# A projection and merge written as one stream, with VectorE, ScalarE and DMA issue pinned to program order

## The chip, the cores and the metric

One Trainium2 chip, one core. The metric is the device time of one launch in microseconds (us), as a median over runs.

## The reference, cut to what matters

One decoder layer, float32, on 1024 prompt rows and 8 x 8 sample rows, which stand together as T = 1088 rows (544, HALF, in each half; 272, CH, in each quarter).

```python
proj = jnp.einsum('bld,de->ble', x, w_in)                 # D = 2048 -> 84 column blocks of 128
gb, gc, h, z_c, q, k, v, z_a, gate_c, gate_a = jnp.split(proj, ...)
conv_out, conv_state = short_conv(gc * h, conv_prev, conv_w)
y_c = silu(z_c) * gb * conv_out
o = window_attention(q, k, v, sinks)      # 128 keys back, ALiBi, 16 heads, 4 kv heads
y_a = silu(z_a) * o
merged = sigmoid(gate_c) * (y_c @ w_conv_out) + sigmoid(gate_a) * (y_a @ w_attn_out)
y = layer_norm(ALPHA * x + merged @ w_out)
```

## The kernel before, in words

Every product is a float32 one in three passes: `split` (L131, L132) takes a tile apart, ScalarE (ACT) casts the high part, VectorE (DVE) subtracts it for the low one, and TensorE (PE) multiplies high by high, high by low and low by high.

A **unit** makes two column blocks of 128 for all rows from one half of the contraction, by a Strassen-Winograd scheme of 7 products (**leaves**). A leaf has 4 **groups** (one for each 128 of the contraction) of 6 matmuls 128x272, so a unit has 28 groups and 168 matmuls. Before a leaf its weights are combined on DVE (L242 to L247) and split; after it `take` adds its sum into the result (DVE, L264) or copies it where it is the first (ACT, L262). The sums of a unit lie in three PSUM tiles called a, c and b; a serves leaves 0, 2, 4 and 6, b serves 3 and 5, so a leaf's `take` has to be done before the leaf that uses its tile again. The side work shares two small PSUM tiles (`aux`).

The order of units: psa0 to psa41 over the first half of x, whose results go to DRAM (pd; psa0 and psa1 together, in `first`, L290 on). Then psb0 to psb41 over the second half, each starting from its loaded pd tile (cb): two for keys and values, eight for queries, nine gates, sixteen for the convolution with gates between them, three gates. Then 16 merge units psm (eight with w_conv_out, whose results go to DRAM as cmd; eight with w_attn_out), each quarter of whose result is multiplied by a gate loaded from sgd (L757); the second eight add the loaded cmd (cmo, L761) and store mgd (L762). Last the product with w_out and the layer norm.

The operands of a set (x0 for psa, x1 for psb, xm0 and xm1 for the merges; the names xa, xb, xm) are made in `Operands`: `load_all` loads four quarters of 4 tiles each (tags a, d, c, b; L165), `combine` makes two sums of them (L182, L183), two more sums follow at L199 and L202, and each leaf's tiles are split. The loads of x1 are issued when unit psa37 begins, those of xm0 and xm1 some units before their first use.

Side work (64 attention steps, one begun every 15 groups; 8 sample steps; the convolution; the gates) is put between groups by `at`, which runs a function when a given group has been written: an attention step is a load, 14 groups later the scores with the whole softmax, 28 the values' load, 30 the transposes, 40 the output. The order on PE is the program's own (`in_order`). On DVE, ACT and the DMA queue of SyncE (SP) it is the tile scheduler's, which takes what it holds to be ready.

Of the kernel before, what the change touches and what calls it, by code (L numbers as in the profile page):

```python
# [50 lines left out]
def tile_hybrid_step(  # L51
# [32 lines left out]


    agenda = {}
    clock = [0]

    def at(step, what):
        assert step >= clock[0]  # L90
        agenda.setdefault(step, []).append(what)

    def tick():
        clock[0] += 1
        for what in agenda.pop(clock[0], ()):
            what()

    last_pe = [None]

    def in_order(ins):  # L100

        if last_pe[0] is not None:
            tc.add_manual_dep(
                ins.ins, last_pe[0].ins.name,
                mybir.DependencyInfo(mybir.DependencyClass.NoSync, mybir.DependencyReason.DATA),
                reason="in_order",
            )
        last_pe[0] = ins

    def matmul(*args, **kw):  # L110
        in_order(nc.tensor.matmul(*args, **kw))  # L111

    def transpose(*args):
        in_order(nc.tensor.transpose(*args))  # L114

    turn_of_sum = [0]

    def sums(name):

        r = turn_of_sum[0]  # L120
        turn_of_sum[0] += 1
        return [
            ps.tile([P, 2, 512], F32, name=f"{name}{s}", tag=f"sum{(r + i) % 3}", bufs=1)
            for i, s in enumerate("acb")
        ]

    def aux(name):
        return ps.tile([P, 512], F32, name=name, tag="ax", bufs=2)
# [6 lines left out]
    nc.vector.memset(eps, LN_EPS)  # L135
# [13 lines left out]
    class Operands:  # L149
# [5 lines left out]
        def __init__(self, stage, name, sources):  # L155
            self.stage, self.name, self.sources = stage, name, sources
            self.x = [[None] * 4 for _ in range(7)]

        def load(self, r, c, tag):

            out = []
            for k, src in enumerate(self.sources):
                t = self.stage.tile([P, HALF], F32, name=f"x{tag}{self.name}{k}{r}{c}", tag=f"x{tag}{k}")
                tc.keep_in_program_order(
                    nc.sync.dma_start(t, src[r][:, c * HALF : (c + 1) * HALF])  # L165
                )
                out.append(t)
            return out

        def load_all(self, between=lambda: None):  # L170
# [4 lines left out]
            self.b22 = self.load(1, 1, "c")  # L175
            self.b12 = self.load(0, 1, "b")

        def combine(self):

            self.t3, self.t2 = self.b12, self.b22  # L180
            for k in range(4):
                nc.vector.tensor_sub(self.t3[k], self.t2[k], self.t3[k])  # L182
                nc.vector.tensor_add(self.t2[k], self.t3[k], self.b11[k])  # L183
            self.b22 = None

        def put(self, i, src):
            for k in range(4):
                o = slot([2, HALF], F32R, f"x{self.name}{i}_{k}")
                split(o[:, 0], o[:, 1], src[k])
                self.x[i][k] = o  # L190

        def step(self, i):

            if i == 2 and self.b22:
                self.combine()
            if i == 4:

                for k in range(4):
                    nc.vector.tensor_sub(self.t3[k], self.b22[k], self.t2[k])  # L199
            if i == 5:  # L200
                for k in range(4):
                    nc.vector.tensor_sub(self.b21[k], self.b21[k], self.t2[k])  # L202
            self.put(
                i,
                (lambda: self.b11, lambda: self.b21, lambda: self.t2, lambda: self.t3,
                 lambda: self.t3, lambda: self.b21, lambda: self.b22)[i](),
            )
            if i == 3:
                self.b22 = self.load(1, 1, "a")

    def enter(x, *units):

        for i in range(7):
            x.step(i)
            for u in units:
                next(u)
        for u in units:
            assert next(u, None) is None
# [5 lines left out]
    def unit(*args):  # L224
        for _ in products(*args):
            pass

    def products(name, src, x, c, add, accs=None, s=None):

        if len(src.shape) == 3:  # L230
            raw = src
        else:
            raw = upool.tile([P, 4, 512], F32, name=f"wr{name}", tag="wr", bufs=2)
            nc.sync.dma_start(raw.rearrange("p a b -> p (a b)"), src)
        a11, a21, a12, a22 = (raw[:, i] for i in range(4))
        if s is None:
            s = upool.tile([P, 2, 512], F32, name=f"ws{name}", tag="ws", bufs=1)
        s1, s2 = s[:, 0], s[:, 1]

        def ready(i):  # L240
            if i == 2:
                nc.vector.tensor_add(s1, a21, a22)  # L242
                nc.vector.tensor_sub(s2, s1, a11)
            if i == 3:
                nc.vector.tensor_sub(a21, a11, a21)
            if i == 6:
                nc.vector.tensor_sub(a12, a12, s2)  # L247
            w = wpool.tile([P, 2, 512], F32R, name=f"w{name}_{i}", tag="w", bufs=5)
            split(w[:, 0], w[:, 1], (a11, a12, s2, a21, s1, a22, a12)[i])
            return w  # L250

        acc_a, acc_c, acc_b = accs or sums(f"ps{name}")
        accs = (acc_a, acc_c, acc_a, acc_b, acc_a, acc_b, acc_a)
        starts = (True, True, False, True, False, False, False)

        def view(f, h):
            return c[:, f, h * HALF : (h + 1) * HALF].rearrange("p (a b) -> p a b", a=2)

        def take(f, h, acc, fresh):
            dst, val = view(f, h), acc[:, :, :CH]  # L260
            if fresh and not add:
                nc.scalar.copy(dst, val)  # L262
            else:
                nc.vector.tensor_add(dst, dst, val)  # L264

        after = (
            (0, 0, acc_a, True), (0, 0, acc_c, False), (1, 0, acc_a, True), (1, 1, acc_b, True),
            (1, 1, acc_a, False), (1, 0, acc_b, False), (0, 1, acc_a, True),
        )
        for i in range(7):  # L270
            w, acc = ready(i), accs[i]
            for k in range(4):
                ks = slice(k * P, (k + 1) * P)
                xo = x[i][k]
                first, last = starts[i] and k == 0, k == 3
                for wi, xi in ((0, 0), (0, 1), (1, 0)):
                    for h in range(2):
                        matmul(
                            acc[:, h, :CH], w[:, wi, ks], xo[:, xi, h * CH : (h + 1) * CH],
                            start=first and wi == 0 and xi == 0, stop=last and wi == 1,  # L280
                            skip_group_check=not starts[i],
                        )
                tick()
            take(*after[i])
            yield


    st = ExitStack()
    stage = pool("stage", stack=st, side="right")
    x0 = Operands(stage, "a", [(xt[k], xt[k + 8]) for k in range(4)])  # L290
    with ExitStack() as first:
        ps0 = pool("ps0", space=PSUM, stack=first)
        fpool = pool("first", stack=first, side="right")
        acc = [ps0.tile([P, 2, 512], F32, name=f"first{i}", tag=f"first{i}") for i in range(4)]

        idle = fpool.tile([P, 2, 512], F32, name="idle", tag="idle")
        nc.vector.memset(idle, 0.0)
        for i in range(WARM):
            matmul(acc[0][:, 0], idle[:, 0, 0:P], idle[:, 0], start=True, stop=True)

        c = [upool.tile([P, 2, T], F32, name=f"ca{p}", tag="c", bufs=2) for p in range(2)]
        raws = []

        def first_weights():
            p = len(raws)
            raws.append(upool.tile([P, 4, 512], F32, name=f"wra{p}", tag="wr", bufs=2))
            nc.sync.dma_start(raws[p].rearrange("p a b -> p (a b)"), win[p, 0])

        x0.load_all(first_weights)
        s1 = fpool.tile([P, 2, 512], F32, name="wsa1", tag="idle")  # L310
        both = [
            products(f"a{p}", raws[p], x0.x, c[p], False, (acc[2 * p], acc[2 * p + 1], acc[2 * p + 1]), (None, s1)[p])
            for p in range(2)
        ]
        enter(x0, *both)
        for p in range(2):
            nc.sync.dma_start(pd[p], c[p])
    ps = pool("ps", space=PSUM)
    x1 = Operands(stage, "b", [(xt[k], xt[k + 8]) for k in range(4, 8)])
# [721 lines left out]
```

## Time and profile before

| | |
|---|---|
| median of 3 runs | 2726.57 us (2725.57 to 2728.25) |
| the profiled execution's own time | 2730.23 us, its span 2728.5 us |
| PE busy | 2635.7 us (97%), 19426 matmuls |
| DVE busy | 1751.0 us (64%) |
| ACT busy | 1076.7 us (39%) |
| DMA | 415.99 MB, mean 152 GB/s |

Busy times are of the profiled execution. PE is busy nearly all the time, and its matmuls are pipelined, so what can be lost or won in it is its idle time and the time in which the chip grants it a lower clock (PEclk, a share of full speed). In the rows of a timeline the first two numbers are the start and the length in us, and a bracket gives the idle time before the instruction and what ended it.

### The profile page before, as it was taken

The page shows a single profiled execution, that of the slowest core. Times are in us where ns is not written, and L with a number is a line of the kernel's source. Part 1 is how long each engine was busy: PE and PEld are TensorE (multiplying, and loading weights), DVE is VectorE, ACT ScalarE, POOL GpSimd, SP SyncE. Part 2 cuts the span into 40 slices and gives each one's busy share as a digit, 9 for nine tenths or more (in the row PEclk, how much of TensorE's full clock was granted, in tenths as well). Part 3 has the DMA queues.
Part 4 walks back from the last instruction along what each step waited for, and adds up shares of the span by engine and source line. Part 5 has one row for each costly group of instructions (what it writes and reads, how often), then busy time and mean ns, then how long its engine had stood idle before and what let it go on. Part 6 is the DMA issues. An engine that isn't in the chain of part 4 may idle for free. (4 is left out here: it accounts for less than half of the span.)

```text
span 2728.5 us, 48044 instructions
## 1 busy us (share of the span) xinstructions
PE 2635.7 (97%) x19426; PEld 2546.2 (93%) x19426; DVE 1751.0 (64%) x3311; ACT 1076.7 (39%) x2070; POOL 0.2 (0%) x4
## 2 busy tenths in 40 slices
PE   7999999999999989989999999999999999899998
PEld 6999999999999989988999999999999999688886
DVE  7444444444445858877878888878866866533836
ACT  4333233332333535556664544554433523322221
POOL 0000000000000000000000000000000000000000
PEclk8999999999999999999999999999999999999999
DMA  4322222222233456665554444445446566733543
GB/s 148 121 104 112 96 96 113 109 98 96 113 124 149 145 180 211 210 192 164 184 180 153 160 150 167 143 157 194 150 163 227 171 235 204 240 100 111 181 144 104
DMA packets 167330, 415.99 MB, mean 152 GB/s; under 512 B 23442, under 2 KB 75666, under 8 KB 139172
## 3 DMA queue, kind: packets, MB, share of 16 engines
q1 hardware_dynamic: 167108, 412.92, 44.3%
q8 instruction: 153, 2.51, 0.4%
q14 instruction: 69, 0.57, 0.1%
HBM read 295.33 MB, written 119.48 MB: 152 GB/s over the span
## 5 line engine op out<-in xcount | busy, mean ns | idle before, releaser
L111 PE MATMUL o<-wo,m 128*128 128x512 f32 x1344 | 320.9, 394 | 0.2 <-DVE r L854 0.2
L111 PEld LDWEIGHTS o<-wo,m 128*128 128x128 f32 x1344 | 255.3, 190 | 55.8 <-issue 0.6
L132 DVE TENSOR_TENSOR wa<-wra,wa 128x512 fp32r<-128x512 f32 x210 | 145.4, 693 | 216.1 <-ACT wa L131 216.1
L131 ACT CAST wb<-wrb 128x512 fp32r<-128x512 f32 x210 | 129.7, 619 | 247.9 <-PE psb3b L111 12.1
L131 ACT CAST wa<-wra 128x512 fp32r<-128x512 f32 x210 | 130.4, 622 | 180.1 <-PE first L111 5.4
L132 DVE TENSOR_TENSOR wo<-wraw,wo 128x512 fp32r<-128x512 f32 x112 | 76.7, 687 | 148.7 <-ACT wo L131 148.6
L131 ACT CAST wo<-wraw 128x512 fp32r<-128x512 f32 x112 | 69.3, 621 | 223.5 <-PE o L111 188.6
L132 DVE TENSOR_TENSOR wb<-wrb,wb 128x512 fp32r<-128x512 f32 x210 | 144.4, 688 | 10.1 <-ACT wb L131 9.1
L132 DVE TENSOR_TENSOR wa<-wsa,wa 128x512 fp32r<-128x512 f32 x84 | 58.2, 693 | 109.9 <-ACT wa L131 109.9
L131 ACT CAST wa<-wsa 128x512 fp32r<-128x512 f32 x84 | 52.3, 623 | 77.8 <-issue 75.1
L132 DVE TENSOR_TENSOR wm<-wrm,wm 128x512 fp32r<-128x512 f32 x80 | 55.3, 693 | 39.8 <-ACT wm L131 39.5
L131 ACT CAST wb<-wsb 128x512 fp32r<-128x512 f32 x84 | 51.8, 617 | 56.4 <-PE psb22a L111 3.6
L131 ACT CAST wm<-wrm 128x512 fp32r<-128x512 f32 x80 | 49.7, 622 | 58.5 <-PE psm_6b L111 4.8
L473 ACT ACTIVATE p<-p,nm 128x256 f32<-128x256 f32 (+1 forms) x128 | 62.4, 488 | 23.0 <-DVE nm L465 22.7
L480 ACT ACTIVATE p<-p,den 128x256 f32<-128x256 f32 (+1 forms) x128 | 56.4, 487 | 29.1 <-DVE den L478 28.4
L111 PEld LDWEIGHTS first<-xa,wa 128*128 128x128 f32 x336 | 48.2, 212 | 17.7 <-DVE xa L132 9.3
L111 PE MATMUL first<-xa,wa 128*128 128x272 f32 x336 | 49.9, 314 | 14.7 <-DVE xa L132 8.4
L757 DVE TENSOR_TENSOR cm<-cm,sg 128x544 f32<-128x544 f32 x64 | 46.1, 723 | 27.6 <-ACT cm L262 20.3
L132 DVE TENSOR_TENSOR wb<-wsb,wb 128x512 fp32r<-128x512 f32 x84 | 57.6, 686 | 9.1 <-ACT wb L131 9.0
L131 ACT CAST pp<-pt 128x512 fp32r<-128x512 f32 (+1 forms) x64 | 35.8, 560 | 59.1 <-PE pt L114 58.5
L459 DVE SCALAR_TENSOR_TENSOR p<-delta,sc 128x256 f32<-128x256 f32 (+1 forms) x128 | 45.7, 397 | 13.4 <-PE sc L111 13.4
L111 PE MATMUL o<-wo,ms 128*128 128x512 f32 x128 | 40.5, 398 | 13.9 <-DVE ms L132 10.7
(1081 smaller groups left out, 6506.8 us busy)
## 6 DMA issues: line engine op xcount, KB each, us to landing
pd<-ca SPq DMA_DIRECT2D x42, 1088.0 KB
cb<-pd SPq DMA_DIRECT2D x42, 1088.0 KB
wra<-in_win SPq DMA_DIRECT2D x42, 1024.0 KB
wrb<-in_win SPq DMA_DIRECT2D x42, 1024.0 KB
wraw<-in_wo SPq DMA_DIRECT2D x128, 256.0 KB
sgd<-cb SPq DMA_DIRECT2D x16, 1088.0 KB
sg<-sgd SPq DMA_DIRECT2D x64, 272.0 KB
qt<-qd SPq DMA_DIRECT2D x128, 128.0 KB
```

The source lines that it names most:

```text
L111: in_order(nc.tensor.matmul(*args, **kw))
L131: nc.scalar.copy(hi, raw)
L132: nc.vector.tensor_sub(lo, raw, hi.bitcast(F32))
L459: nc.vector.scalar_tensor_tensor(p[:, e, :nk], delta[:, 2 * P - nk :], SLOPES[2 * j + e], sc[:, e, :nk], op0=ALU.mult, op1=ALU.add,)
L473: nc.scalar.activation(p[:, e, :nk], p[:, e, :nk], AF.Exp, bias=nm[:, e : e + 1], accum_out=den[:, e : e + 1],)
L480: nc.scalar.mul(p[:, e, :nk], p[:, e, :nk], den[:, e : e + 1])
L757: nc.vector.tensor_mul(c[:, f, hs], c[:, f, hs], sg)
```

## The change

What it does:

- Four wrappers (`te`, `ve`, `se`, `dq`) issue everything up to the product with w_out, and chain each instruction to the one before it on its engine: PE, DVE, ACT and SP's DMA issue are all in program order.
- All units from psa0 to psm's last are one list of (unit, leaf), walked by one loop (`run`). In leaf g: after group 0 the `take` of leaf g-1; after group 1 the weights' sums and casts of the leaf 3 ahead; after group 2 the next unit's raw weights (in leaf 0) or its result tile and pd load (in leaf 4); after group 3 the weights' low parts.
- The next operand set is made as pieces in a list `line`, of which each group takes one (two in the first two units). A set's leaf is split as soon as the last unit of the set before has done with that leaf. `ahead_of` issues a set's loads and puts the four pairs of its combination on `line` in the same moment: for x1 when psa37 begins, for xm0 when gate 13 begins, for xm1 in merge unit 4.
- Side work has fixed groups: of an attention step load 0, scores 14, bias 16, maximum 17, exponents 19, sums 22, values' load 22, scaling 23, transposes 27, high 29, low 30, output 34, then 36, 37 and 38. Long DVE instructions are cut in halves (some 68 more). The convolution's first tap goes from DVE to ACT. The sample step's loads are issued 12 groups before its first product.
- In the first two units leaves 0 and 1 of psa0 come before those of psa1; then they alternate. On DVE the last row of leaf 2's operands (xa split from xca) is now the 33rd behind the memsets, and was the 51st.
- In the merge, gate tiles are fetched one or two leaves ahead into two buffers; the weight tiles of the last stage have three buffers and had four.

```diff
+    te, ve, se, dq = (InOrder(e) for e in (nc.tensor, nc.vector, nc.scalar, nc.sync))
     def tick():
         clock[0] += 1
         for what in agenda.pop(clock[0], ()):
             what()
+        for _ in range(pieces[0]):
+            if line:
+                line.pop(0)()
-    def split(hi, lo, raw):
-        nc.scalar.copy(hi, raw)
-        nc.vector.tensor_sub(lo, raw, hi.bitcast(F32))
+        def combine(self, k):
+            line.append(lambda: ve.tensor_sub(self.t3[k], self.t2[k], self.t3[k]))
+            line.append(lambda: ve.tensor_add(self.t2[k], self.t3[k], self.b11[k]))
+            for k in range(4):
+                u.products(i, k)
+                if k == 0:
+                    settle()
+                if k == 1:
+                    todo = make_high(g + 1 + ahead(g), 2)
+                if k == 2 and nxt and i == u.loads_next and nxt.raw is None:
+                    nxt.load()
+                if k == 2 and nxt and i == 4 and nxt.c is None:
+                    nxt.room()
+                if k == 3:
+                    for v, n in todo:
+                        v.low(n)
+                tick()
+            pending[0] = (u, i)
+            if u.ops.leaves and u.ops.leaves[0] is u:
+                u.ops.leaves[1].put(i)
+    stream = [(u, i) for u in both for i in range(2)] + [(u, i) for i in range(2, 7) for u in both]
+    def ahead_of(ops):
+        ops.load_all()
+        for k in range(4):
+            ops.combine(k)
+            for dt, what in (
+                (0, self.load), (14, self.scores), (16, self.biased), (17, self.maximum),
+                (19, self.exponents), (22, self.sums), (23, self.normed), (22, self.load_values),
+                (27, self.turn), (29, self.high), (30, self.low), (34, self.output),
+                (36, self.half), (37, self.joined), (38, self.gated),
+            ):
+                at(t + dt, what)
```

How it moves instructions, at two places. In the names, wa is a weight tile split for a psa unit (its second number is the leaf), wra and wsa are the raw weights and their sums, ca is a unit's result, xbb and xcb are x1's loaded tiles of tags b and c.

DVE where x1 is combined, in unit psa37; before:

```order
L264 TENSOR_TENSOR ca_8077<-ca_8077,psa37c 128x544
L132 TENSOR_TENSOR wa_6_8256<-wra_8078,wa_6_8256 128x512
L132 TENSOR_TENSOR wa_0_8292<-wra_8286,wa_0_8292 128x512
L132 TENSOR_TENSOR wa_1_8320<-wra_8286,wa_1_8320 128x512
L247 TENSOR_TENSOR wra_8286<-wra_8286,wsa_8288 128x512
L264 TENSOR_TENSOR ca_8077<-ca_8077,psa37a 128x544
L132 TENSOR_TENSOR wa_2_8350<-wsa_8288,wa_2_8350 128x512
L182 TENSOR_TENSOR xbb_8061<-xcb_8053,xbb_8061 128x544
L182 TENSOR_TENSOR xbb_8063<-xcb_8055,xbb_8063 128x544
L183 TENSOR_TENSOR xcb_8053<-xbb_8061,xab_8037 128x544
```

The first xbb row stood behind the takes of leaf 1 (psa37c) and leaf 4 (psa37a) of psa37.

DVE at the same place, now:

```order
L97 TENSOR_TENSOR xbb_8076<-xcb_8068,xbb_8076 128x544
L97 TENSOR_TENSOR wra_7868<-wra_7868 128x512
L97 TENSOR_TENSOR xcb_8068<-xbb_8076,xab_8052 128x544
L97 TENSOR_TENSOR xbb_8078<-xcb_8070,xbb_8078 128x544
L97 TENSOR_TENSOR wa_3_8101<-wra_7868,wa_3_8101 128x512
L97 TENSOR_TENSOR xcb_8070<-xbb_8078,xab_8054 128x544
L97 TENSOR_TENSOR xbb_8080<-xcb_8072,xbb_8080 128x544
L97 TENSOR_TENSOR xcb_8072<-xbb_8080,xab_8056 128x544
L97 TENSOR_TENSOR xbb_8082<-xcb_8074,xbb_8082 128x544
L97 TENSOR_TENSOR wa_4_8135<-wsa_8032,wa_4_8135 128x512
L97 TENSOR_TENSOR xcb_8074<-xbb_8082,xab_8058 128x544
L97 TENSOR_TENSOR ca_7983<-ca_7983,psa37c 128x544
```

The first xbb row has moved ahead of psa37's take of leaf 1, and the sum wra that leaf 3's weights need (the row after it) and leaf 3's low part (wa_3) stand behind it.

SP where the sample outputs are stored (out_k_p to out_v_s) in the first sample steps; before:

```order
L437 DMA qt_6_12359<-qd_146 64x512 x2
L420 DMA szd_160<-sz_12125 128x1024
L439 DMA kt_6_12362<-ksd_137 128x256
L411 DMA qd_152<-qa_12116 64x8x128 x2
L411 DMA qd_152<-qb_12117 64x8x128 x2
L360 DMA cb_12515<-pd_74 128x2176
L587 DMA sbias_0_12139<-in_sbias 32x136
L589 DMA skt_0_12141<-in_ckt 64x4x128
L595 DMA sva_0_12144<-in_cv 128x4x64
L558 DMA out_k_p<-kl 128x256
L562 DMA out_k_s<-kn 8x256 x2
L507 DMA yd_114<-o_3_12256 128x128
```

The operands of step 6 (qt_6, kt_6), which its scores need 14 groups later, were issued before the outputs.

SP there, now:

```order
L97 DMA vt_4_12349<-vcd_141 128x256
L97 DMA szt_4_12351<-szd_154 128x128
L97 DMA yd_114<-o_3_12344 128x128
L97 DMA out_k_p<-kl 128x256
L97 DMA out_v_p<-vlast 128x256
L97 DMA out_k_s<-kn 8x256 x8
L97 DMA out_k_s<-in_ck 8x2x15360
L97 DMA out_v_s<-vn 8x256 x8
L97 DMA out_v_s<-in_cv 8x2x15360
L97 DMA qt_6_12464<-qd_146 64x512 x2
L97 DMA kt_6_12467<-ksd_137 128x256
```

Of them qt_6 and kt_6 now come behind all the outputs, the two copies of 8x2x15360 (in_ck, in_cv) among them.

## Rows read from the trace of the kernel before

**Rows 1.** The page: span, busy time by engine, chain of waits by engine.

```profile
span 2728.5 us, 48044 instructions
PE 2635.7 (97%) x19426; PEld 2546.2 (93%) x19426; DVE 1751.0 (64%) x3311; ACT 1076.7 (39%) x2070; POOL 0.2 (0%) x4
PE 12%; DMA 2%; DVE 1%; ACT 0%; issue 0%; SPq 0%; DVEq 0%; ACTq 0%
```

**Rows 2.** Windows: stretch, length, busy (count) by engine, PEclk, DMA share, GB/s.

```profile
60.00:893.00 833.00, 833.00 (x6637) 833.00 (x6636) 384.28 (x563) 251.69 (x433) 0.00 (x0) 1.00 0.29 110
945.00:1200.00 255.00, 235.59 (x1847) 233.00 (x1846) 188.74 (x396) 131.74 (x266) 0.00 (x0) 0.97 0.64 195
1200.00:1420.00 220.00, 212.26 (x1656) 203.38 (x1655) 175.75 (x503) 140.01 (x325) 0.00 (x0) 0.98 0.54 180
1420.00:1945.00 525.00, 517.03 (x4111) 513.18 (x4110) 432.69 (x897) 248.69 (x517) 0.00 (x0) 1.00 0.48 165
```

**Rows 3.** Timeline of PE, then of DVE, in the first two units.

```profile
33.28 1.73 PE L111 MATMUL first<-xa,wa 128*128 128x272 f32 x6 [6.15 <-DVE xa L132]
39.01 21.19 PE L111 MATMUL first<-xa,wa 128*128 128x272 f32 x145 [2.09 <-DVE xa L132]
...
18.77 0.69 DVE L132 TENSOR_TENSOR wa<-wsa,wa 128x512 fp32r<-128x512 f32 x1
45.84 0.74 DVE L132 TENSOR_TENSOR xa<-xba,xa 128x544 fp32r<-128x544 f32 x1
```

**Rows 4.** Timeline of SP and DVE: x1's loads in psa37, xm1's in the merge.

```profile
809.30 0.32 SPq L323 DMA_DIRECT2D pd<-ca  x1
809.67 3.16 SPq L165 DMA_DIRECT2D xab<-in_xt  x4
825.04 1.35 DVE L182 TENSOR_TENSOR xbb<-xcb,xbb 128x544 f32<-128x544 f32 x2
...
2081.37 3.19 SPq L165 DMA_DIRECT2D xam<-yd  x4
2096.70 1.45 DVE L182 TENSOR_TENSOR xbm<-xcm,xbm 128x544 f32<-128x544 f32 x2 [0.64 <-DMA xbm<-yd]
```

**Rows 5.** Timeline of PE: stalls at x1's entry and in the query and sample steps.

```profile
925.80 4.75 PE L111 MATMUL psb0a<-xb,wb 128*128 128x272 f32 x24 [3.36 <-DVE cb L264]
995.86 3.25 PE L111 MATMUL psb3a<-xb,wb 128*128 128x272 f32 x24 [3.28 <-DVE cb L264]
1007.24 1.12 PE L111 MATMUL sc<-kt,qt 128*128 128x128 f32 x4 [5.87 <-DMA qt<-qd]
1181.50 1.08 PE L111 MATMUL sps<-skt,sqs 64*32 64x136 f32 x4 [6.53 <-DMA skt<-in_ckt]
```

**Rows 6.** Timeline of SP around the sample outputs.

```profile
1177.26 0.50 SPq L558 DMA_DIRECT2D out_k_p<-kl  x1
1183.81 8.05 SPq L562 DMA_DIRECT2D out_v_s<-vn  x8
1199.34 0.33 SPq L439 DMA_DIRECT2D kt<-ksd  x1
```

**Rows 7.** Timeline of PE: waits for the shared small sums in the sample steps.

```profile
1260.15 0.40 PE L111 MATMUL spo<-spn,vn 32*64 32x128 f32 x2 [1.60 <-DVE o L503]
1294.92 1.23 PE L111 MATMUL sc<-kt,qt 128*128 128x256 f32 x4 [2.53 <-ACT so L652]
```

**Rows 8.** Timeline of PE: entries of xm0 and of xm1.

```profile
1964.32 3.25 PE L111 MATMUL psb25b<-xb,wb 128*128 128x272 f32 x24 [2.43 <-DVE cb L264]
2142.64 3.28 PE L111 MATMUL psm_7a<-xm,wm 128*128 128x272 f32 x24 [2.80 <-DVE cm L264]
```

**Rows 9.** Timeline of DVE, SP and PE at the merge's end.

```profile
2322.20 0.72 DVE L761 TENSOR_TENSOR cm<-cm,cmo 128x544 f32<-128x544 f32 x1 [1.35 <-DMA cmo<-cmd]
2328.86 0.33 SPq L905 DMA_DIRECT2D gB<-in_ln_g  x1
2323.21 1.19 PE L111 MATMUL o<-wo,ms 128*128 128x512 f32 x2 [7.77 <-DVE ms L132]
```

More of the change, by code (lines that the diff above doesn't have):

```diff
@@ L192, in step @@
[L192 to L206, printed above, removed]
-            )
-            if i == 3:
-                self.b22 = self.load(1, 1, "a")
@@ L211, in enter @@
[L211 to L285, printed above, removed]
@@ L288, in tile_hybrid_step @@
[L288 to L317, printed above, removed]
@@ L355, in tile_hybrid_step @@
[L355 to L371 removed]
+            self.t2 = self.load(1, 1, "c")
@@ new lines, in tile_hybrid_step @@
+    stage_st = ExitStack()
+    stage = pool("stage", stack=stage_st, side="right")
+    x0 = Operands(stage, "a", [(xt[k], xt[k + 8]) for k in range(4)])
+    first = ExitStack()
+    ps0 = pool("ps0", space=PSUM, stack=first)
+    fpool = pool("first", stack=first, side="right")
+    acc = [ps0.tile([P, 2, 512], F32, name=f"first{i}", tag=f"first{i}") for i in range(4)]
+    idle = fpool.tile([P, 2, 512], F32, name="idle", tag="idle")
+    ve.memset(idle, 0.0)
+    for i in range(WARM):
+        te.matmul(acc[0][:, 0], idle[:, 0, 0:P], idle[:, 0], start=True, stop=True)
@@ new lines, in tile_hybrid_step, with others @@
+    both = [
+        Unit(f"a{p}", win[p, 0], x0, end=lambda c, p=p: dq.dma_start(pd[p], c)) for p in range(2)
+    ]
+    rest = iter(both)
+    x0.load_all(lambda: next(rest).load())
+    for p, u in enumerate(both):
+        u.accs = (acc[2 * p], acc[2 * p + 1], acc[2 * p + 1])
+    both[1].loads_next = 5
+    both[1].s = fpool.tile([P, 2, 512], F32, name="wsa1", tag="idle")
+    x0.put(0)
+    x0.put(1)
+    def others():
+        x0.put(2, x0.combine)
+        for i in range(3, 7):
+            x0.put(i)
@@ new lines, in output, with heads @@
+        def output():
+            po = box["po"] = aux(f"spo{n}")
+            te.matmul(po[0:64, 0:P], vn[new, g // 2, half], pn[new], start=True, stop=False)
+            for b in range(NH):
+                c = slice(b * 32, (b + 1) * 32)
+                te.matmul(po[0:64, c], va[:, b, :], pa[:, c], start=False, stop=b == NH - 1)
+        def heads():
+            pov = box["po"][0:64, 0:P].rearrange("p (b h t) -> p b h t", b=NH, h=4)
+            for h in range(4):
+                e = h % 2
+                se.copy(o[64 * e : 64 * e + 64, h // 2], pov[:, :, h, :])
@@ new lines, in gated @@
+        def gated():
+            for jj in range(2):
+                j = 2 * g + jj
+                z = szs[:, j, new]
+                ve.tensor_mul(z, z, o[:, jj].rearrange("p b t -> p (b t)"))
+                if hb:
+                    dq.dma_start(yd[8 + j][:, 0:TS], szs[:, j, :])
+        for dt, what in (
+            (9, rows), (12, lambda: scores(0)), (15, lambda: scores(2)), (18, maximum), (20, exponents),
+            (24, sums_), (25, lambda: normed(0)), (26, lambda: normed(2)),
+            (27, lambda: turn(0)), (28, lambda: turn(1)), (29, lambda: turn(2)), (30, lambda: turn(3)),
+            (31, turn_new), (34, output), (36, heads), (38, gated),
+        ):
+            after(dt, what)
@@ L725, in tile_hybrid_step @@
-        for ct in range(8):
-            conv(ct)
-            if ct == 7:
-                at(clock[0] + 4, lambda: conv_state(0))
-                at(clock[0] + 8, lambda: conv_state(1))
-            if ct % 2:
-                gate(9 + ct // 2)
-    assert not agenda
-    keep.close()
-    mp = pool("merge", side="right")
-    st = ExitStack()
-    stage = pool("mstage", stack=st, side="right")
-    def branch(b):
-        x = Operands(stage, f"m{b}", [(yd[8 * b + k], yd[8 * b + k + 4]) for k in range(4)])
-        x.load_all()
-        x.combine()
-        return x
@@ new lines, in tile_hybrid_step, with gate_unit, samples, open_conv @@
+    for j in range(8):
+        project(QZ + j, lambda c, j=j: asked(j, c))
+    def gate_unit(d, begin=None):
+        return project(GT + d, lambda c: gate(d, c), begin)
+    def samples(i):
+        if i == 0:
+            heads_st.close()
+            open_samples()
+        sample(i // 2, i % 2)
+    for i in range(8):
+        gate_unit(i, lambda i=i: after(16, lambda: samples(i)))
+    gate_unit(8)
+    def open_conv():
+        sam.close()
+        pools["conv"] = cp = pool("conv", stack=con)
+        late["pts"] = cp.tile([18, 8, P], F32, name="cst")
@@ new lines, in tile_hybrid_step, with mix, open_merge @@
+    for ct in range(8):
+        project(CV + 2 * ct, lambda c, ct=ct: convolved(ct, c), (lambda: after(24, open_conv)) if ct == 0 else None)
+        def mix(c, ct=ct):
+            mixed(ct, c)
+            if ct == 7:
+                after(4, lambda: conv_state(0))
+                after(8, lambda: conv_state(1))
+        project(CV + 2 * ct + 1, mix)
+        if ct % 2:
+            gate_unit(9 + ct // 2)
+    mst = ExitStack()
+    xm = [None, None]
+    def open_merge():
+        con.close()
+        keep.close()
+        pools["merge"] = pool("merge", side="right")
+        stage = pool("mstage", stack=mst, side="right")
+        for b in range(2):
+            xm[b].stage = stage
+        ahead_of(xm[0])
```

921 lines of the change are left out of this document (565 added, 356 removed).

## The prediction

> **What bounds the kernel now.** I read the page first [rows 1]: PE is busy 2635.7 of 2728.5 us and leads the chain of waits, so the change can win only what PE loses: its idle time and the time at the low clock. It adds no matmul and takes none away.
>
> The windows show where PE loses [rows 2]. From 60 to 893 us 6637 matmuls take 833.00 us: 0.1255 us each, 3.01 us for a leaf of 24 matmuls, 0.753 for a group of six, no loss. In the second half I count as lost the idle time and the clock's deficit: 945 to 1200 us loses 19.4 + 0.03 x 255 = 27 us, 1200 to 1420 us 7.7 + 0.02 x 220 = 12 us, 1420 to 1945 us 8 us. That is 47 us beside the attention, the samples and the convolution. The rest I read in the timeline of PE with the releaser of each wait: the first two units wait for split operands [rows 3], and the entry of each new operand set for DVE's takes [rows 5, 8]; at the merge's end PE waits 7.77 us for ms [rows 9].
>
> The price of a wait: a leaf's 24 matmuls behind an idle time of 3.36 us took 4.75 us and not 3.01 [rows 5], so the clock adds 1.7 us to a wait of some length.
>
> **First two units.** DVE is the limit: from 18.77 to 45.84 us it starts 45 instructions, 0.62 us each [rows 3]. The last operand of leaf 2 comes 18 instructions sooner in its order, so up to 18 x 0.62 = 11 us. PE waits 6.15 and 2.09 us there for such operands [rows 3]; I take both and a little low clock, **8.5 us** won. If the later leaves' operands then come late, 4; at most 11.
>
> **Entry of x1 and of xm0.** Splitting one piece per group, as the last unit of the old set gives its slots back, spreads what came in a burst. At psb0 the wait was 3.36 us with 1.7 of clock [rows 5]: I take 4 of it. At xm0's entry the wait shown is 2.43 us [rows 8] with the clock behind it: 3. Together **7 us** won (2 to 9).
>
> **Queries, samples, convolution.** Psb3 waits 3.28 us for a take and 5.87 for its qt; the first sample step 6.53 us for skt [rows 5]. With two clock prices that is 19 of the 27 us. Skt is now issued 12 groups ahead, at least 9 us; the qt load stands behind fewer stores. I let all three go and 3 us of smaller waits, **22 us** (8 to 25).
>
> Against this stands SP's order. All stores of the sample outputs now come ahead of qt and kt of step 6. Before, SP began them at 1177.26 us, spent 8.05 us on one group of eight alone, and issued the next kt at 1199.34 us [rows 6]: 22 us. The step's scores come 14 groups later, 10.5 us and with side work some 14. So PE waits 22 - 14 = 8 us and pays 1.7 of clock: **9.7 us** lost (0 if the stores flow faster, 13 if the side work is thin).
>
> The other waits of the sample steps are for the small sums that scores, transposes and samples share, 1.60 and 2.53 us for example [rows 7]. Fixed groups don't add tiles, so they stay: 1 us won of 12. In the convolution the long instructions are halved and a tap moves to ACT: 4 of 8 us (0 to 6). **5 us** together.
>
> **The loads of a set with their combination right behind.** Here the change adds a wait. Before, x1's loads are issued at 809.67 us and DVE comes to the first combination at 825.04, where it waits for nothing [rows 4]; it had meanwhile done the takes of psa37's leaves 1 and 4. Now this combination is DVE's in the second group of psa37. What it will wait for shows in the merge: xm1's loads are issued at 2081.37 us and the first combination starts at 2096.70, released by the load [rows 4]. That is 15.3 us. Behind it stand leaf 3's weight sum, then ACT's cast of it, in all 2 us. SP issues the loads behind the store of the unit before, so about 1 us into the unit, and leaf 3 is due 3 x 3.01 us into it: PE waits 15.3 + 2 - 8 = 9 us, and 1.7 for the clock: **11 us** lost for x1 (0 if the tiles land within 6 us, 13 at most).
>
> In gate 13 the nearest thing ahead of xm0's loads that waits is a pd load some three leaves earlier, so SP can issue them up to 8 us before the unit: the first tiles are there 15.3 - 8 = 7 us into it. Takes are all DVE's there; leaf 0's, behind the combination and some 4 us of other DVE work, ends at 11.3, and leaf 2 needs its tile at 2 x 3.01 = 6.0: 5.3 us and the clock, **7 us** lost (0 to 13). For xm1 SP can run further ahead: **2 us** (0 to 8). [...]
>
> **Merge and end.** At xm1's entry PE waited 2.80 us for a take [rows 8]; in the merge DVE has 64 gate products that it now reaches at fixed groups, some before the gate tile lands. I take **4 us** lost (0 to 9). The last sum waited 1.35 us for cmo at 2322.20, and the loads behind it start with gB at 2328.86 [rows 9]; with that tile fetched leaves ahead and the low parts of ms done sooner, the store goes out sooner: **4.7 us** won of PE's 7.77 (1 to 6).
>
> What costs nothing: some 68 more half instructions on DVE, about 0.62 us each, 42 us of busy time over the kernel, are covered by its idle share of 36% [rows 1]; without that cover they would be paid in the stretch of 945 to 1200 us, where DVE is at 188.74 of 255 us [rows 2]. One weight buffer fewer in the last stage is covered by the two loads still in flight.
>
> **The sum.** Won: 8.5 + 7 + 22 + 5 + 4.7 = 47.2. Lost: 9.7 + 11 + 7 + 2 + 4 = 33.7. Net 13.5 us won. The profiled execution took 2730.23 us, 3.7 over the median of 2726.57; 13.5 less gives 2716.7 beside the profile and **2713 us** as a median. A measurement can tell about 0.2%, 5.5 us, from no change. This case alone reaches from 2700 to 2727.
>
> **Rivals.**
> (a) *The fixed order takes nearly all waits away.* For it: in 60 to 893 us the same units run without any loss [rows 2], so a program whose side work always comes in time would lose nothing; DVE has slack. The 47 us shrink to 6, and DVE's and SP's waits are absorbed by the weights made three leaves ahead: 8.5 + 7 + 41 + 4.7 = 61 us won, 2665; with half of the absorption 2685. Against it: the 15.3 us of a load [rows 4] are longer than three leaves. [...]
> (b) *Slower: head of line on DVE.* Place: the three combinations behind their loads. If each wait goes through in full, 15.3 + 2 us less the two leaves of 6 us until the first sum tile is needed again, with the clock 13 us each, they cost 39 in place of 20, and DVE's backlog then delays the takes; if, besides, the 22 us won beside the attention come down to 5 because DVE now waits at fixed places for ACT's exponents, the kernel is at 2726.6 - 13.5 + 19 + 17 = 2749, or near 2738 with half. It turns to slower once the three cost over 33 us. For it: 15.3 us is measured. Against: SP runs ahead where its stores don't wait.
> (c) *No difference.* PE is 97% busy, and the scheduler's order was near what the fixed order is; the gains of the start are given back at the combinations: 2721 to 2732.
>
> **How the numbers follow.** The forecast gets 0.46 (most of it faster, 0.08 of it within 0.2%), (a) 0.25, (b) 0.23, (c) 0.06 (0.05 of it within 0.2%). Faster by over 0.2%: 0.64; within: 0.13; slower: 0.23. The range for 8 in 10 goes from the middle of (a) to the near half of (b): 2672 to 2742. The bounds above, put together, would reach further on both sides, but they don't all fall on one side at once.
>
> **What the profile would show.** Right: psa2 begins 8 to 9 us sooner; in psa37 the first xbb combination on DVE has an idle time of some 12 us released by a load, and PE stops before leaf 3 for 9 us; scores of step 6 in the first sample steps wait for qt or kt by 8 us; no wait for skt. Wrong: no wait in psa37 (then (a) gains), or waits in all three combinations of over 10 us on PE (then (b)). It would also be wrong if waits for shared small sums grow to several us for each attention step, which no term above has.

## The result and the profile after

The changed kernel takes 2747.32 us (median of 5 runs, 2742.78 to 2749.23) against 2728.25 us of the kernel before beside it: a ratio of 1.006 (95% interval 1.0041 to 1.008). It is slower by 0.6%, where 2713 us was forecast: the sign was wrong and the time outside the range.

The page of the changed kernel (span, busy time by engine, chain of waits by engine):

```profile
span 2747.1 us, 47820 instructions
PE 2646.6 (96%) x19426; PEld 2548.5 (93%) x19426; DVE 1756.7 (64%) x3371; ACT 1058.9 (39%) x2074; POOL 0.2 (0%) x4
PE 73%; DVE 14%; ACT 6%; DMA 5%; issue 2%; SPq 1%; DVEq 0%; ACTq 0%
```

Against [rows 1] the span is 18.6 us longer and the busy times nearly the same. The two chains can't be set side by side: that of before adds up to 15%, for it could be followed back only to the last 412 us of the span, while this one covers all of it.

Where the time went shows when each unit's time on PE is taken less 21.1 us (168 matmuls at the 0.1255 us of the lossless stretch [rows 2]) and less some 0.4 to 4.7 us for the side work's own matmuls, from their shortest rows. What is left is lost. Summed by stretch, in us, from the PE timelines:

| stretch | before | change | difference | forecast |
|---|---|---|---|---|
| first two units | 17.6 | 11.4 | -6.2 | -8.5 |
| psa37 (x1's loads) | 0 | 14.7 | +14.7 | +11 |
| psa41, psb0 (x1's entry) | 7.4 | 6.0 | -1.4 | -4 |
| psb1 to psb11 | 29.1 | 15.2 | -13.9 | -12.3 |
| psb12 to psb18 (samples) | 14.1 | 21.7 | +7.6 | -1 |
| psb26 to psb22 (convolution) | 15.8 | 13.5 | -2.3 | -4 |
| psb23 (xm0's loads, gate 13) | 0 | 9.3 | +9.3 | +7 |
| psb25, psm_0 (xm0's entry) | 7.7 | 6.5 | -1.2 | -3 |
| psm_4 (xm1's loads) | 0 | 7.2 | +7.2 | +2 |
| last psm_7 of w_conv_out, next psm_0 (xm1's entry) | 3.8 | 8.3 | +4.5 | +4 |
| from the last merge unit to the end | 434.3 | 435.5 | +1.2 | -4.7 |

The forecast's -12.3 is its 22 less 9.7. Each entry rests on ideal times and is good to about 1 us.

The windows of a stretch without loss and of those with the new losses, to set beside [rows 2] (length, busy time and count by engine, PEclk, DMA share, GB/s):

```profile
60.00:800.00 740.00, 740.00 (x5896) 740.00 (x5895) 327.76 (x493) 221.57 (x388) 0.00 (x0) 1.00 0.30 105
800.00:838.00 38.00, 26.33 (x188) 26.11 (x187) 15.73 (x25) 6.99 (x13) 0.00 (x0) 0.82 0.48 175
1219.00:1420.00 201.00, 189.69 (x1460) 178.52 (x1458) 162.59 (x463) 119.26 (x290) 0.00 (x0) 0.99 0.50 161
1900.00:1931.00 31.00, 23.92 (x174) 23.73 (x174) 17.05 (x27) 6.56 (x10) 0.00 (x0) 0.89 0.67 252
2063.00:2093.00 30.00, 24.37 (x184) 24.15 (x184) 18.08 (x29) 6.76 (x13) 0.00 (x0) 0.94 0.76 280
```

In psa37 (800 to 838 us) PE, DVE and ACT are all idle together, and 188 matmuls take 38 us. The timeline there, rows of SP, DVE, ACT and PE:

```profile
803.11 3.12 SPq L97 DMA_DIRECT2D xab<-in_xt  x4
811.43 2.46 SPq L97 DMA_DIRECT2D xbb<-in_xt  x4
814.29 0.33 SPq L97 DMA_DIRECT2D wra<-in_win  x1
...
817.17 0.72 DVE L97 TENSOR_TENSOR xbb<-xcb,xbb 128x544 f32<-128x544 f32 x1 [14.57 <-DMA xbb<-in_xt]
817.81 0.68 DVE L97 TENSOR_TENSOR wra<-wra 128x512 f32<-128x512 f32 x1
824.19 0.71 DVE L97 TENSOR_TENSOR ca<-ca,psa37c 128x544 f32<-128x544 f32 x1
...
818.58 0.62 ACT L97 CAST wa<-wra 128x512 fp32r<-128x512 f32 x1 [15.87 <-DVE wra L97]
819.11 0.60 ACT L97 COPY ca<-psa37a 128x544 f32<-128x544 f32 x1
...
819.76 5.81 PE L97 MATMUL psa37a<-xa,wa 128*128 128x272 f32 x24 [11.67 <-ACT ca L97]
```

One chain is to be read here. DVE stands 14.57 us for the load. Right behind come the sum wra, whose cast ACT waits for 15.87 us, and behind that cast ACT's take of leaf 0 (ca from psa37a). Leaf 2 needs that tile, so PE stops two leaves into the unit for 11.67 us; its leaf then takes 5.81 us, where a leaf of 24 matmuls at the full clock has rows of 3.17 us. PE had stood still, and the clock granted in the six us behind that was 0.50 (PEclk):

```profile
820.00:826.00 6.00, 6.00 (x27) 6.00 (x28) 5.97 (x10) 1.14 (x3) 0.00 (x0) 0.50 0.14 56
```

Of the 14.7 us lost, 3.0 lie behind the wait. The forecast had the first half of this chain and stopped PE one leaf later, at leaf 3's weights. In [rows 4] the same first combination began at 825.04 without a wait.

DVE kept to the program's order here: the take of psa37c began at 824.19 us, with leaf 1's sum complete since the start of the 11.67 us in which PE stood, because the 14.57 us of the wait, and then 7 us of work that stood ahead of it in the fixed order, came first.

### The profile page after: what moved, and what is told of

The parts are those of the page before. It is cut to its first block, busy times and chain, and to the rows that moved or that the text cites. A ratio compares the mean times of both kernels' runs of the same rounds, so it can differ in the third digit from the quotient of the medians.

```text
span 2747.1 us, 47820 instructions
## 1 busy us (share of the span) xinstructions
PE 2646.6 (96%) x19426; PEld 2548.5 (93%) x19426; DVE 1756.7 (64%) x3371; ACT 1058.9 (39%) x2074; POOL 0.2 (0%) x4
## 4 chain that ended last, share of the span: by engine, by line
PE 73%; DVE 14%; ACT 6%; DMA 5%; issue 2%; SPq 1%; DVEq 0%; ACTq 0%
PE o L97 11%; DVE cb L97 2%; DVE wb L97 1%; DMA yr<-mgd 1%; ACT wb L97 1%; ACT p L97 1%; DMA wraw<-in_wo 1%; PE psm_5a L97 1%; PE psm_1a L97 1%; PE psm_6a L97 1%; PE psm_2a L97 1%; ACT L97 1%; PE psm_4a L97 1%; DVE nm L97 1%; DVE wsb L97 1%
## 5 line engine op out<-in xcount | busy, mean ns | idle before, releaser
L97 ACT CAST wm<-wsm 128x512 fp32r<-128x512 f32 x32 | 19.9, 621 | 104.2 <-DVE wsm L97 98.4
L97 PE MATMUL first<-xa,wa 128*128 128x272 f32 x336 | 47.8, 305 | 10.2 <-ACT wa L97 4.3
L97 DVE TENSOR_TENSOR o<-po,ot 64x128 f32<-64x128 f32 x128 | 36.0, 281 | 24.5 <-ACT ot L97 23.4
```

What stands on the lines that cost most here:

```text
L97: first = f(*args, **kw)
```

## The experiments

Two theories at the start. A: with the engines pinned, what stands behind a waiting instruction waits too, and PE stops where a set's loads are put. B: the loads' own traffic or their place is what costs. For the samples it was open whose order counts. Each run with several repetitions is given against the kernel before on the same chip; the others are a single run each, and stand on their timelines.

**The combination later.**

```diff
         ops.load_all()
-        for k in range(4):
-            ops.combine(k)
+        def combined():
+            for k in range(4):
+                ops.combine(k)
+        after(22, combined)
```

> Edit: the three combinations (x1, xm0, xm1) are put in line 22 groups after their loads, not in the same moment; all else as in the change. Theory A (DVE in program order waits for the loads at the combination, and all behind it waits too): the waits of 11.67, 7.08 and 5.63 us at psa37, psb23 and psm_4 go, and with them the losses of 14.7, 9.3 and 7.2 us, so about 31 us less than the change: 2716, some 12 us under before. Rival B (the traffic of 4.4 MB per operand set, or the place of the loads in SP's order, holds up PE there): the stalls stay, 2747. Rival C (the wait only moves to where the combination now stands): PE loses over 5 us in the next unit, 2730 to 2740.

It gave 2734.28 us, a ratio of 1.0017 (1.0006 to 1.0028). Xm0's loss went from 9.3 to 0.9 us, but psa37 kept 7.4 and psm_4 went from 7.2 to 9.2 with its neighbours. That is neither A nor B as first put. The total is in rival C's range, but not by its mechanism: the combinations wait for nothing, and the unit after psa37 loses nothing. The DVE timeline, in psa37 and in psm_4:

```profile
824.26 0.69 DVE L97 TENSOR_TENSOR wa<-wra,wa 128x512 fp32r<-128x512 f32 x1 [10.53 <-ACT wa L97]
825.50 0.72 DVE L97 TENSOR_TENSOR xbb<-xcb,xbb 128x544 f32<-128x544 f32 x1
...
2064.58 0.72 DVE L97 TENSOR_TENSOR cm<-cm,sg 128x544 f32<-128x544 f32 x1 [11.03 <-DMA sg<-sgd]
```

The combinations no longer wait. Now the next item that needs a later transfer does: the cast of psa38's raw weights, issued behind 16 tiles of x1 (ACT stands 8.11 us for that load), and in the merge a gate tile. Theory A had to be widened: all that stands behind the loads, on SP and then on DVE and ACT.

**The loads spaced.** A quarter of a set at 4, 10, 16 and 22 groups, the combination at 44.

```diff
-        ops.load_all()
-        for k in range(4):
-            ops.combine(k)
+        def quarter(name, r, c, tag):
+            setattr(ops, name, ops.load(r, c, tag))
+        for dt, what in ((4, ("b11", 0, 0, "a")), (10, ("b21", 1, 0, "d")), (16, ("t2", 1, 1, "c")), (22, ("t3", 0, 1, "b"))):
+            after(dt, lambda what=what: quarter(*what))
...
+        after(44, combined)
```

> Edit: each set's loads are issued a quarter at a time, 4, 10, 16 and 22 groups into the unit, so that the next unit's raw weights (group 2) and the gate tiles stand ahead of most of them, and the combination is put in line 44 groups in; all engines stay pinned. Theory A in its wider form (with pinned queues whatever stands behind a transfer of 4.4 MB waits: the combination in the change; in the run with the combination 22 groups later the next unit's weight cast, 7.4 us at psa37, and the gate product, 8.7 us at psm_4): none of the three places loses over 1.5 us, the sum of the three from 31 to under 4, total 2716 to 2720. Rival B (loads of this size cost PE by their traffic): the three still lose 15 us or more together, 2730.

2715.73 us, 0.9954 (0.9939 to 0.9969): 31.6 us under the change and faster than before, with every engine still pinned. The three places lose 0, 0 and 0.4 us. Windows of psa37 and of psb23:

```profile
802.00:840.00 38.00, 38.00 (x305) 38.00 (x304) 19.45 (x30) 12.59 (x22) 0.00 (x0) 1.00 0.65 232
1900.00:1931.00 31.00, 31.00 (x250) 31.00 (x249) 21.23 (x33) 6.67 (x10) 0.00 (x0) 1.00 0.58 219
```

The same bytes, in psa37 at more GB/s than in the change (232 against 175), in psb23 at fewer (219 against 252), and PE loses nothing. Against B speaks the kernel before as well: it issues the same 16 loads in one go in psa37, and PE goes through without a pause:

```profile
808.00:838.00 30.00, 30.00 (x242) 30.00 (x241) 19.15 (x29) 9.28 (x16) 0.00 (x0) 1.00 0.69 259
```

So B is out as far as it means traffic: 259 GB/s cost PE nothing where no engine that feeds it waited for the loads. The loads' place in SP's order does count; that is part of the widened A.

**SP free.**

```diff
     te, ve, se, dq = (InOrder(e) for e in (nc.tensor, nc.vector, nc.scalar, nc.sync))
+    dq = nc.sync
```

> Edit: SP's DMA issue alone is given back to the scheduler's order, DVE, ACT and PE stay pinned. Theory A: DVE still meets the combination in the second group, so psa37 keeps over 10 us; the sample outputs' stores no longer stand just ahead of step 6's qt and kt, so psb11 falls from 7.8 to about 3; total 2738 to 2744. Rival (SP's fixed order is the main cost): the total falls under 2730.

2725.77 us: the rival's side, and my expectation missed. DVE still meets the combination at the head of psa37, but it waits for nothing, and psa37 and psm_4 lose 0; psb23 keeps 9.0 us. The DVE timeline in psa37:

```profile
803.09 0.72 DVE L97 TENSOR_TENSOR xbb<-xcb,xbb 128x544 f32<-128x544 f32 x1
```

The scheduler had issued the loads of x1's tiles xab from 49.6 us on, over 750 us ahead. So it takes both: SP's pinned issue puts the loads late, DVE's pinned order meets them early. Freeing either all but cures psa37 (0 and 2.1 us lost). Psb11 lost 3.7 us, where about 3 was foreseen. The price of SP's freedom was psb1 to psb9, 14.5 us lost and not 4.7.

**DVE free, and ACT free.**

```diff
+    ve = nc.vector
```

> Edit: DVE alone is given back to the scheduler's order; ACT, SP and PE stay pinned. Theory A: the scheduler puts the combination behind psa37's take of leaf 4 as in before, so psa37 loses nothing and the total falls by 14.7 us at the least, 31 if the scheduler moves all three. In the sample steps (psb11 to psb18, 29.5 us lost in the change, 16.9 before), if DVE's fixed order is what costs there, 10 us less; if it is ACT's order or SP's stores, they stay at 27 to 30. Rival B: psa37 keeps 14 us.

2698.22 us, 49 under the change and 31 under before. Losses at the three places: 2.1, 0.9 and 0 us; psb12 to psb18 10.1; xm1's entry 4.9 and not 8.3. Theory A held, and of the samples' loss over half is DVE's order.

```diff
+    se = nc.scalar
```

> Edit: ACT alone is given back to the scheduler's order. Theory A: the three combinations keep their losses (14.7, 9.3, 7.2 us), since DVE is what waits. If ACT's fixed order (exponents and table loads ahead of the weights' casts) costs in the sample steps, psb11 to psb18 fall from 29.5 to about 17 us and xm1's entry from 8.3 to 4; if not, within 2 us of the change: 2747.

2732.73 us. Psb12 to psb18 fell to 13.8 and the convolution from 13.5 to 9.0, psa37 to 10.2, psm_4 to 4.6; psb23 stayed at 9.6. Xm1's entry did not fall (10.3), which was a miss. In psa37 PE now stops one leaf later:

```profile
820.61 5.12 PE L97 MATMUL psa37b<-xa,wa 128*128 128x272 f32 x24 [8.16 <-ACT wa L293]
```

ACT's take of leaf 0 is no longer held up by the cast, and PE waits 8.16 us for leaf 3's weights. That is the forecast's wait, 9 us there, and its 11 us are 10.2. The other 4.5 us of psa37 in the change are the price of ACT's fixed order.

**Both free.**

```diff
+    ve, se = nc.vector, nc.scalar
```

> Edit: DVE and ACT are both given back to the scheduler's order. DVE alone gave 2698.2, ACT alone 2732.7, against 2747 for the change (one look each). If what each costs is apart: 2684. If they are two ends of the same waits (DVE waits for ACT's casts and the reverse), freeing ACT as well adds little: 2693 to 2698. psb12 to psb18: 10.1 us with DVE free, 13.8 with ACT free, 21.7 in the change; 5 with both if they add.

2769.28 us, slower than any other version; nothing like it was expected. The convolution stretch lost 56.7 us and not 13.5. PE's waits there:

```profile
PE pt L97 <- ACT p L652: 28.7, 13, 4.1
```

The transposes of the attention steps, pinned on PE, waited 28.7 us in 13 cases for ACT's scaled probabilities (columns: us in total, times, longest). With either engine's order fixed, that softmax came in time: ACT fixed and DVE free lost 11.8 us in the stretch, DVE fixed and ACT free 9.0.

**The sample outputs' stores split.**

```diff
-        after(10, store)
+        after(13, store)
+        after(28, lambda: window(vn, cv, v_s))
```

(`store` now writes the keys alone, `window` one of the two.)

> Edit: the sample outputs' stores are split: keys 13 groups into the sample's opening (just behind an attention step's loads), values 15 groups later (behind the next step's), where the change has both at 10, just ahead of qt and kt. Theory A: the wait of 4.52 us before the scores in psb11 goes, psb11 loses 3 us and not 7.8, and the total falls by 4 to 6 us. Rival B (the wait there is DVE's, as its releaser tn says): psb11 stays within 1.5 us of 7.8.

2742.28 us, at the low end of the change's own five times (2742.78 to 2749.23), so the total shows nothing; psb11 lost 3.7 us and not 7.8. In the change, SP's and PE's timelines read:

```profile
1183.83 8.28 SPq L97 DMA_DIRECT2D out_v_s<-vn  x8
1192.15 0.70 SPq L97 DMA_DIRECT2D out_v_s<-in_cv  x1
1192.96 1.14 SPq L97 DMA_DIRECT2D qt<-qd  x2
...
1203.04 1.19 PE L97 MATMUL sc<-kt,qt 128*128 128x256 f32 x4 [4.52 <-DVE tn L97]
```

With the stores split, the wait before these scores was gone, and DVE's tn is made only after them (1202.47 us, the scores at 1199.65). In four other runs in which the stores stay where the change has them, the same scores wait too, 1.2 to 4.2 us, and there the row names the load; with the loads spaced, for one:

```profile
1189.29 1.20 PE L97 MATMUL sc<-kt,qt 128*128 128x256 f32 x4 [4.23 <-DMA kt<-ksd]
```

So in the change the row named DVE where it was the transfer, and A holds. The wait was priced at 9.7 us with its clock and measured 4.52, or about 4 us of psb11.

**The low parts of the weights later.**

```diff
                 if k == 3:
-                    for v, n in todo:
-                        v.low(n)
+                    if g >= 14 and g + 4 < len(stream):
+                        owed += todo
```

(`owed` is worked off after the next leaf's first group.)

> Edit: all engines pinned as in the change; the low parts of a leaf's weights are made on DVE one leaf later than their casts' group 3, after the next leaf's first group, so that ACT's cast has two groups more. In psb12 to psb18 DVE stood 13.4 us in 13 waits for just these casts in the change. Theory D (DVE's fixed order costs in the sample steps because DVE stands for ACT's casts with takes queued behind): psb12 to psb18 fall from 21.7 to under 16 us, the total by 5 to 10. Rival E (DVE's work is at fixed groups in bursts there, and the waits for casts only take up slack): psb12 to psb18 stay within 2 us of 21.7. Both leave psa37, psb23 and psm_4 as in the change.

2754.14 us, 1.0082 (1.0061 to 1.0102). Waits of DVE in psb12 to psb18 in the change, the largest first:

```profile
DVE wb L97 <- ACT wb L97: 13.4, 13, 2.4
DVE o L97 <- ACT ot L97: 4.9, 3, 2.8
```

and with this edit:

```profile
DVE o L97 <- ACT ot L97: 7.1, 5, 2.2
DVE pp L97 <- ACT pp L97: 6.0, 4, 1.9
```

The 13.4 us of waits for casts left the list and the stretch lost 25.3 us, 3.6 more than in the change: theory D fell. Those waits had taken up slack, as rival E has it, though E's 2 us were exceeded.

**All pinned, loads spaced and stores split.** The two edits above together.

> Edit: all engines pinned as in the change, the loads spaced with the combination 44 groups in, the stores split. The spaced loads alone gave 2715.7 and the stores alone 5 us: if they add, 2709 to 2712. What is then left over the version with DVE free (psb12 to psb18 at 21 us against 10, psm_0 at 8.3 against 4.9, the first units) is the price of DVE's fixed order itself, 15 us or more.

2716.6 us, 0.9953 (0.9937 to 0.9968), no faster than the spaced loads alone (0.9954): the few us of the stores did not show in the medians (psb11 gained 3.1 us on them, psb12 to psb18 lost 1.5). Psb12 to psb18 lost 23.2 us. This is the base of the next two runs.

**One DVE chain, or part of it free.** First the side work's DVE instructions are given back to the scheduler, then the units'.

```diff
-                ve.tensor_reduce(nm, self.p[:, :, : self.nk], axis=AX.X, op=ALU.max)
+                nc.vector.tensor_reduce(nm, self.p[:, :, : self.nk], axis=AX.X, op=ALU.max)
...
```

(In the first run so for all DVE instructions of attention, samples, queries, convolution and gates; in the second for those of `Unit`.)

> Edit: on top of the version with spaced loads and split stores (all pinned, 2716.6), the DVE instructions of the side work (attention, samples, queries, convolution, gates) are given back to the scheduler; those of the units (weights, takes) and of the operands stay in one fixed chain. Theory F (the side work's fixed groups put DVE instructions where they wait, with the units' takes and weight sums behind): psb12 to psb18 fall from 23.2 to about 10 as with DVE wholly free, total 2700 to 2704. Theory G (the fixed place of the units' own instructions, takes after group 0 and weight sums after group 1, is what costs): they stay at 20 or more.

> Edit: the reverse on the same base: the units' DVE instructions (weight sums, low parts, takes) go to the scheduler, the side work and the operands stay in one fixed chain. Theory F: psb12 to psb18 stay at 20 or more, for the side work still waits in its chain ahead of them unless the scheduler slips units' work between; theory G: they fall to about 10 and xm1's entry from 8.3 to 5, total 2696 to 2704. If both runs fall to about 10, it is neither chain but their being one chain.

2701.23 and 2707.30 us; psb12 to psb18 lost 11.0 and 11.8. Windows of that stretch: the change, then the two runs:

```profile
1219.00:1419.00 200.00, 188.69 (x1452) 177.52 (x1450) 161.59 (x462) 118.27 (x289) 0.00 (x0) 0.99 0.50 162
```

```profile
1200.00:1390.00 190.00, 185.57 (x1456) 176.29 (x1455) 158.94 (x462) 117.32 (x288) 0.00 (x0) 1.00 0.53 172
```

```profile
1196.00:1387.00 191.00, 186.28 (x1458) 176.59 (x1457) 159.47 (x462) 118.66 (x289) 0.00 (x0) 1.00 0.53 171
```

DVE does the same work, some 160 us, in 10 us less. So it is neither the side work's order nor the units', but that both stand in one chain: a unit's take then waits behind a side instruction that isn't ready, and the reverse. PE's waits in the stretch show both kinds; in the change, the largest:

```profile
PE sps L97 <- DVE pp L97: 2.1, 2, 1.1
PE psb18b L97 <- DVE cb L97: 1.9, 1, 1.9
PE sc L97 <- issue: 1.3, 1, 1.3
PE sc L97 <- DVE st L97: 1.1, 3, 0.7
```

All told they are 3.8 us for takes (cb) and 5.9 for the side work's tiles, of 11.0; before, 6.0 us, all for the side work's tiles and none for takes. In the two runs all of PE's waits there are 4.3 and 4.4 us. Freeing the units cost in the convolution (23.9 us lost, 13.4 on the base).

**The fastest: DVE free, loads spaced, stores split.**

> Edit: DVE alone free (ACT, SP and PE pinned), the sets' loads spaced with the combination 44 groups in, the sample stores split: the candidate for the fastest. DVE free alone: 2698.2, of which psa37 still loses 2.1 us and psb10 with psb11 8.9. Theory A: the spacing takes psa37's 2 us and the stores 3 to 4 us of psb11's: 2692 to 2694, 1.2 to 1.3% under before. If the scheduler, given other load times, orders DVE worse elsewhere (as it did with ACT free too), 2700 or more.

2693.04 us, 0.9862 (0.9839 to 0.9884), as expected and the fastest version run. Psa37, psb23 and psm_4 lose nothing, psb10 and psb11 5.6 us, psb12 to psb18 9.5. The same edits with ACT free as well:

> Edit: DVE and ACT free, the loads of the sets spaced with the combination 44 groups in, and the sample stores split: the candidate for the fastest. With DVE free the three places lost 3 us together and psb10 with psb11 8.9, of which the stores should give 4: 4 to 7 us under the run with DVE and ACT free; 2688 to 2692 if that is at 2695.

2768.07 us, 1.0142 (1.0125 to 1.0159): the convolution's loss, 61.6 us, was there again, and the expectation fell with that of both free.

**Three weight buffers in the kernel before.**

```diff
-        raw = mq.tile([P, 512], F32, name="wraw", tag="wraw", bufs=4)
+        raw = mq.tile([P, 512], F32, name="wraw", tag="wraw", bufs=3)
```

> Edit: the kernel before with three weight buffers in the last stage and not four, as the change has. The prediction costed this at nothing: 2726 to 2730, the stretch from the last merge unit's start to the end at 434 us. If the buffer matters, that stretch grows by over 3 us.

2734.58 us, 1.0018 (1.0006 to 1.0031), and the stretch from the last merge unit to the end 438.5 us against 434.3 in one profiled execution each. By the interval the buffer is worth 2 to 8 us. Its trace shows where: PE waits for the last weights (l), in this run and in the change, and not at all in the kernel before. This run, then the change:

```profile
PE o L111 <- DVE l L132: 1.4, 4, 0.8
PE o L111 <- ACT l L131: 0.5, 1, 0.5
...
PE o L97 <- DVE l L1079: 1.4, 4, 0.7
PE o L97 <- ACT l L1078: 0.6, 1, 0.6
```

Of the 4.2 us by which this run's profile is longer there, these waits are 1.9, and another 1.9 are longer waits for ms. The change has less waiting for ms in that stretch (6.5 us in two waits, of them 4.90 at its start, against 10.7 and 7.77 before [rows 9]) and 1.1 us more for the residual rows. So gain and loss nearly cancel. The change with four buffers was not run.

## Why the prediction was wrong, step by step

Two steps failed most: the 20 us for the three combinations, where the wait is right and its size isn't (31.2 us), and the 1 us won in psb12 to psb18, where the one fixed DVE chain cost 7.6. By term:

- **First two units**: right in kind, 6.2 us won where 8.5 was taken; psa2 begins 6.6 us sooner and not 8 to 9.
- **The clock's price** of 1.7 us a wait set a row's length (4.75) against a leaf's spacing (3.01); rows at the full clock are 3.17 and begin 3.01 us apart. In psa37 3.0 us were lost behind the wait of 11.67.
- **Entries of x1 and xm0**: 7 taken, 2.6 measured. The work is spread as foreseen, but at psb0 PE now waits 2.35 us for a cast of xb, and at psm_0 2.85 us for ACT's take, which stands behind ACT's operand casts and two gate activations.
- **Queries and first samples, with the stores**: 12.3 net taken, 13.9 measured. The waits for skt and for psb3's qt went. The stores' price was too high (4 and not 9.7): the 22 us read in [rows 6] from SP's first store to the next kt held other loads as well, and that kt was a later step's, for step 6's stood ahead of the stores. In the change the stores took SP 13.5 us (1179.31 to 1192.85).
- **Samples, psb12 to psb18**: "Fixed groups don't add tiles, so they stay: 1 us won" failed in sign. 7.6 us were lost, since the price of one DVE chain for units and side work was in no term. The waits for the shared small sums did stay in total (6.0 and 5.9 us); what came new were PE's waits for takes, 3.8 us, and a wait of 1.3 us that no row explains; the clock was not lower (0.99 in 1219 to 1419 us, 0.98 before in 1228 to 1419). The two runs with part of the chain free show it: 11.0 and 11.8 us lost and not 23.2.
- **The three combinations**: the mechanism and its three places were right, the size was not: 31.2 us for 20. Psa37 was 14.7 for 11: PE stopped at leaf 2 and not at leaf 3, because ACT's take stood behind the cast, and the clock cost more (3.0 us and not 1.7). With ACT free PE stopped at leaf 3, and 10.2 us were lost. Xm0 was 9.3 for 7, with its first combination 8.7 us into the unit and not 7. Xm1 was 7.2 for 2: SP did not run far enough ahead. It issued xm1's loads at 2060.01 us, 4 us ahead of the unit, because four gate loads for two buffers had held it from 2045.39 to 2059.95.
- **Merge and end**: xm1's entry was lost as priced (4.5). The 4.7 us won at the end did not come: 4.2 us of waits for ms went, but "one weight buffer fewer in the last stage is covered" was wrong by 2 to 8 us (run with the kernel before, not with the change).
- **Halved instructions at no cost**: not tried by itself.

The sum missed by 32 us: 11 at the combinations, 8.6 at the samples, 5.9 at the end, the rest in gains that were too large. No one of these alone turns 13.5 us won into 19 lost. The outcome is rival (b) by its mechanism, but not by its threshold: it was to decide from 33 us at the three places, and 31 sufficed because other gains were smaller. Its "near 2738 with half" is the middle between no change and 2749; half of its two added losses, 18 us, gives 2731.

What stays open: why the scheduler, with both DVE and ACT free, lets the softmax come late, which pairs of instructions in the one chain cost the most beside the samples, and why xm0's place keeps 9.0 us with SP free. The halves of the DVE instructions and the tap on ACT have no run of their own.

## What to carry to other kernels

When an engine's order is fixed by hand, an instruction that depends on a load belongs in the order where the load has surely landed, and the loads' own issue has to be looked at with it: here four megabytes issued in one go held up the next weights too, and spacing them, with the combination later, gained 31 us. Pinning an engine that serves both the main stream and side work made each wait for the other here, some 12 us in the sample steps; leaving DVE, or a part of its work, to the scheduler kept the gains of the fixed order. Two fixed chains side by side were not run. After moving one wait, look in the timeline for the next one behind it before counting the gain.

## What the runs showed that was not expected

The eight 8 KB stores of the values took SP 8.28 us in the change, right behind a copy of 960 KB between DRAM tensors, and 3.29 us in the run with the stores split, where that copy had been issued 13.7 us before. It is not the stores that are slow. Seven of them were issued in 2.6 us; the eighth, which is the eighth DMA behind the copy, waited for the copy itself:

```profile
SPq L97 <- DMA out_k_s<-in_ck: 5.4, 1, 5.4
```

SP's DMAs take turns on eight semaphores in this trace (1125 of 1133 come back to the one of eight issues before), and this store waited on the copy's. So here the copy held up, by 5.4 us, the DMA that SP issued eight places behind it.

And the releaser that a wait is put down to can be an engine that was only the last to signal: the scores' wait of 4.52 us stood under DVE's tn and went with the stores.
